# Unbroken reciprocal-root chains in the norms, one chain for the final norm, and paced reloads of expert activations, in a two-block transformer kernel

## The chip, the cores and the metric

The kernel runs on one core of one Trainium2 chip. The metric is the device time of one execution in microseconds; the median over several runs is the number compared.

## What is computed

Two blocks run one behind the other on 256 tokens of width 1024, in float32. The first has an mLSTM with a sliding-window attention beside it ("mix"), a cross attention to a memory ("cross") and a layer of 16384 experts with product keys ("peer"), and ends with a norm. The second has an "even" mixer (stick-breaking attention and retention), a convolutional feed-forward layer ("ffn0"), an "odd" mixer (gated linear attention) and a second feed-forward layer ("ffn1"). The parts that matter here, cut short:

```python
def rms_norm(x, g):
    y = xf * lax.rsqrt(jnp.mean(xf * xf, axis=-1, keepdims=True) + EPS)
    return (y * g).astype(x.dtype)

def peer_ffn(...):                       # per block of tokens, all 16384 experts by product keys
    u = expert_down[eidx]
    a = gelu(einsum('thkd,td->thk', u, xb))
    return einsum('thk,thkd->td', g * a, expert_up[eidx])

def first_block(...):
    h = h + peer_ffn(rmsnorm(h, g_ffn[l]), ...)
    return rmsnorm(h, g_final)           # the final norm

def second_block(...):
    hn = rms_norm(h, mix_norm_g[layer])  # a norm directly behind the final norm
    mix = even_mixer(hn, ...)            # p = hn @ w_in; qa = rms_norm(to_heads(sb_q), q_gain); ...
    h = h + mix
    hn = rms_norm(h, ffn_norm_g[layer])
    h = h + conv_ffn(hn, ...)
```

## The kernel before

**Weights.** Every weight matrix is cut into pieces of 512 KB, 533 of them. For each piece the SP queue issues one DMA into a tile `raw` (L423), ACT rounds it into `hi` (L438), and DVE writes the rest `raw - hi` into `lo` (L439). PE then does three matmuls for each product (`mm3`, L448 to L450: `hi` by the high part of the activations `xh`, `hi` by their low part `xl`, `lo` by `xh`; `out_step`, L586 to L588, does the same for output projections). A piece is 24 matmuls of 128x256, or 12 of 128x512 where tokens are the rows of the result. A piece lives in one of 3 weight buffers in the expert stage and of 6 in the later stages.

**Order.** A scheduler (the Tile framework) reorders the instructions of each engine; on the chip each engine runs its own list strictly in that order. `issue_after(ins)` binds instructions to stand behind `ins`.

**Norms.** A norm isn't applied to the activations before the projection; the projection runs on unscaled activations, and its results are scaled by `r`, one factor for each token. So the projection starts while `r` is still being found: squares on ACT and DVE, `sums` on PE (L200), `rsqrt` on DVE (L461 to L478: ten small operations, `rs_m` to `rs_y`), then for the stages that need `r` along the row `spread` on PE (L213, written `tp<-ident,rs_y`) and a copy on ACT (`xR`, L215). `columns` (L202) starts the sums and the chain, a few pieces into the projection; `rows` does the spread.

**The final norm** (`Final.columns`, L290) stands between the expert stage and the even stage and needs two factors: `rf` for the final norm, and `r` for the norm behind it. Two chains run one behind the other, with three multiplications between and after them.

**The even stage** computes seven projections of four pieces each (`proj_a`, 128x512 matmuls). `ev_qk` scales the first two (`y`), takes a norm by heads (`hns`, then one more chain), and defers `turn`, four transposes on PE and a copy `sb`, by `5 + t` pieces. Eight operations `x.residual(k)` (`h<-h,g,fR`) apply the final norm to `h`. There are eight PSUM banks: four named `acc`, four named `tp`. A `proj_a` takes two `acc` banks.

**The expert stage** first multiplies by `expert_down` (128 pieces), then by `expert_up` (128 pieces). While the routing is being worked out, the first 110 activations are written to memory (`store`, 55 transfers of 256 KB); in the second half they are read back (`u<-store`, L1248) and multiplied onto the routing weights (`ga<-ga,u`, L1249). The pairs of activations that were never stored come first. At the start of the second half SP also issues two single loads: `h<-spill` (1 MB, L1229) and the constants `c_late` (1089 KB, L625).

Of the kernel before, what the change touches and what calls it, by code (L numbers as in the profile page):

```python
# [10 lines left out]
F32 = mybir.dt.float32  # L11
# [6 lines left out]
ALU = mybir.AluOpType  # L18
# [3 lines left out]
P = 128  # L22
# [128 lines left out]
class Norm:  # L151
# [50 lines left out]
    def columns(self):  # L202
        ps = self.b.tp()
        self.sums(ps, "s", 0)
        self.r2 = self.b.rsqrt(ps[:, :2], 2, 1.0, keep=self.tag)
        self.r = [self.r2[:, t:t + 1] for t in range(2)]

# [48 lines left out]
class Final(Norm):  # L256
# [32 lines left out]
    def columns(self):  # L289
        b, nc = self.b, self.b.nc  # L290
        ps = b.tp()
        self.sums(ps, "s", 0)
        self.sums(ps, "f", 2)
        self.rf = b.rsqrt(ps[:, :2], 2, 1.0, keep="f")
        q = b.sp.tile([P, 2], F32, tag="fq", name="fq")
        nc.vector.tensor_mul(q, ps[:, 2:4], self.rf)
        nc.vector.tensor_mul(q, q, self.rf)
        r = b.rsqrt(q, 2, 1.0, keep=self.tag)
        nc.vector.tensor_mul(r, r, self.rf)
        self.r2 = r  # L300
        self.r = [r[:, t:t + 1] for t in range(2)]
# [70 lines left out]
class Builder:  # L372
    def __init__(self, tc, nc, A, out, stages=None):
        self.tc, self.nc, self.A, self.out = tc, nc, A, out
        self.stages = stages
        self.flip = 0
        self.gate = None
        self.free = 100
        self.later = []
        self.mark = None  # L380
        self.apart = []

# [32 lines left out]
    def weight(self, ap, width=D, parts=1):  # L415
        nc = self.nc
        i = self.wn % sum(n for _, n in self.wps)
        self.wn += 1
        wp, bufs = self.wps[0] if i < self.wps[0][1] else self.wps[1]
        raw = wp.tile([P, D], F32, tag="raw", name="raw", bufs=bufs)  # L420
        cuts = [slice(i * width // parts, (i + 1) * width // parts) for i in range(parts)]
        for c in cuts:
            nc.sync.dma_start(raw[:, c], ap[:, c])  # L423
        hi = wp.tile([P, D], F32R, tag="hi", name="hi", bufs=bufs)
        if wp not in self.apart:
            self.apart.append(wp)
            self.skip(wp, 128, "apart")
        lo = wp.tile([P, D], F32R, tag="lo", name="lo", bufs=bufs)
        with ExitStack() as ctx:
            if self.gate:  # L430
                self.free -= 1
                if self.free < 0:
                    for ins in self.gate:
                        ctx.enter_context(self.tc.issue_after(ins))
                if self.free < -4:
                    self.gate = None
            for c in cuts:
                nc.scalar.activation(hi[:, c], raw[:, c], AF.Copy)  # L438
                nc.vector.tensor_sub(lo[:, c], raw[:, c], hi[:, c].bitcast(F32))  # L439
        return hi, lo  # L440
# [17 lines left out]

    def rsqrt(self, ss, n, inv, keep=None):
        sp, v = self.sp, self.nc.vector  # L460
        ms = sp.tile([P, n], F32, tag="rs_m", name="rs_m")  # L461
        v.tensor_scalar(ms, ss, inv, EPS, op0=ALU.mult, op1=ALU.add)
        gi = sp.tile([P, n], I32, tag="rs_g", name="rs_g")
# [12 lines left out]
        out = sp.tile([P, n], F32, tag="rk_" + keep if keep else "rs_y", name="rs_y")  # L476
        v.tensor_mul(out, p, z)
        return out  # L478
# [7 lines left out]

    def proj_a(self, x, aps, width, evac):
        kk = D // width
        n = aps.shape[0]
        accs = [self.acc() for _ in range(2)]  # L490
        for p in range(n):
            wh, wl = self.weight(aps[p])
            for j in range(kk):
                k = p * kk + j
                for t in range(2):
                    sl = (slice(None), k, slice(t * P, (t + 1) * P))
                    cs = slice(j * width, (j + 1) * width)
                    self.mm3(accs[t][:, :width], x.hi[sl], x.lo[sl], wh[:, cs], wl[:, cs], k == 0, k == n * kk - 1)
            x.tick()
            self.step()  # L500
            if p < n - 1:
                yield
        for t in range(2):
            evac(t, accs[t][:, :width])
        yield
# [115 lines left out]

    def consts(self, names, arr):
        n = sum(CONST_COLS[k] for k in names)
        t = self.cp.tile([P, n], F32, tag=arr, name=arr)
        self.nc.sync.dma_start(t, self.A[arr])  # L625
        o = 0
        for k in names:
            self.c[k] = t[:, o:o + CONST_COLS[k]]
            o += CONST_COLS[k]

    def masks(self, pool, tmp, *names):
# [20 lines left out]
    def build(self):  # L652
# [17 lines left out]
        with ExitStack() as ctx:  # L670
            self.sp = self.pool(ctx, "small", bufs=2)
            self.psp = self.pool(ctx, "psum", space=PSUM)
            self.skip(self.pool(ctx, "gaps"), 64)
            self.xu = self.pool(ctx, "xu", bufs=1)
# [411 lines left out]
    def peer(self, xu, base, cw, cx, cq, late, spill, nxt):  # L1086
        nc, A = self.nc, self.A
        mm = nc.tensor.matmul
        with ExitStack() as ctx:
# [138 lines left out]
            self.h = self.pool(late, "h2", side="right").tile([P, 8, T], F32, tag="h", name="h")  # L1228
            nc.sync.dma_start(self.h, spill)  # L1229
            self.cp = self.pool(late, "c_late", side="right")  # L1230
            self.consts(LATE, "c_late")
            u1 = self.xu.tile([P, 8, T], F32R, tag="uh", name="u3")
            order = [j for j in range(0, P, 2) if j >= kept] + [j for j in range(GA, P, 2) if j < kept]
            order += [j for j in range(0, GA, 2) if j < kept]
            coef = {}

            def step(n):
                j = order[n // 2]
                if n % 2 == 0:
                    if j < GA and cg is not None and "x" not in coef:  # L1240
                        coef["x"] = True
                        cg.close()
                        self.skip(self.pool(late, "gapq2", side="right"), 64)
                        self.xq = self.pool(late, "xq2", side="right")
                    src = gslice(j, 2)
                    if j < kept:
                        a = acts_next()
                        nc.sync.dma_start(a.rearrange("p i t -> p (i t)"), store[j // 2])  # L1248
                        nc.vector.tensor_mul(src, src, a)  # L1249
                    i = 4 * (n // 2 % 2)  # L1250
# [111 lines left out]
    def even(self, x, nxt):  # L1362
        nc, A, c = self.nc, self.A, self.c
        mm = nc.tensor.matmul
        with ExitStack() as ctx:
# [9 lines left out]
            qk = [mp.tile([P, 4, T], F32, name="sb%d" % i) for i in range(2)]  # L1375

            def ev_qk(which):
                def f(t, ps):
                    y = mt.tile([P, 8, 64], F32, tag="y", name="y")
                    self.copy_r(y, ps.rearrange("p (h d) -> p h d", h=8), x.r[t])  # L1380
                    r = self.head_norm(mt, y, 8, 64, "hn")
                    nc.vector.tensor_mul(y, y, r[:, :, None].to_broadcast([P, 8, 64]))
                    y = y.rearrange("p h d -> p (h d)")
# [8 lines left out]

                    self.defer(5 + t, turn)
                return f
# [30 lines left out]
            for k in range(8):  # L1425
                self.defer(12 + 2 * k, lambda k=k: x.residual(k))
            self.run(self.proj_a(x, A["even_in"][1], 512, ev_qk(1)))
            self.run(self.proj_a(x, A["even_in"][2], 512, lambda t, ps: self.copy_r(sv[:, t], ps, x.r[t])))

# [326 lines left out]
```

## Time and profile before

| what | value |
|---|---|
| median of 3 runs | 1691.09 us |
| lowest and highest run | 1686.33 and 1693.12 us |
| the profiled execution's own time | 1694.88 us |
| its span | 1693.1 us |
| mean granted TensorE clock of the span | 0.990 |
| PE busy | 1642.2 us, 97% |
| DVE busy | 1261.4 us, 75% |
| ACT busy | 874.0 us, 52% |
| DMA, mean over the span | 188 GB/s |

PE, DVE, ACT and SP are TensorE, VectorE, ScalarE and SyncE. Busy times are shares of the span; the span is the profiled part of the execution, and the execution's own time is a little longer. Line numbers (L439) are those of the kernel before.

### The profile page before, as it was taken

To read this page: it belongs to the slowest core of one execution; us is meant where nothing else is said; L and a number is where in the kernel's file an instruction comes from. 1 tells how busy PE (TensorE), PEld (TensorE's weight loads), DVE (VectorE), ACT (ScalarE), POOL (GpSimd) and SP (SyncE) were. 2 spreads that over 40 slices of the span, in tenths; PEclk is the share of its full clock that TensorE was granted. 3 is DMA by queue.
4 is the path that set the end of the run, shared out by engine and by line. 5 is a ranking of instruction groups with operands and counts; after the bars stand their busy time and mean duration, and the time that the engine had idled before them with its cause. 6 is when DMAs were issued, how large, how long until landed. Compare 5 with 4: busy or idle time off the path is not lost.

```text
span 1693.1 us, 33034 instructions
## 1 busy us (share of the span) xinstructions
PE 1642.2 (97%) x13220; PEld 1561.2 (92%) x13220; DVE 1261.4 (75%) x2504; ACT 874.0 (52%) x1358; POOL 1.3 (0%) x16
## 2 busy tenths in 40 slices
PE   7999999999999999989999999899999999999999
PEld 7879899899999999988999998678999997799998
DVE  7686669998799985677655556877777775677775
ACT  6445455546555655444444445455555565455553
POOL 0000000000000000000000000000000000000000
PEclk9999999999999999999999999899999999999999
DMA  8433544567555555888655555433455545245551
GB/s 280 143 109 121 177 168 150 188 226 272 186 194 203 197 194 199 305 300 301 208 193 197 191 197 204 178 133 109 155 198 189 197 162 176 101 163 198 189 199 63
DMA packets 97516, 318.02 MB, mean 188 GB/s; under 512 B 11842, under 2 KB 13506, under 8 KB 96851
## 3 DMA queue, kind: packets, MB, share of 16 engines
q1 hardware_dynamic: 89154, 301.39, 51.9%
q10 hardware_dynamic: 8208, 14.52, 2.3%
q8 instruction: 104, 1.70, 0.4%
q14 instruction: 50, 0.40, 0.1%
HBM read 299.36 MB, written 16.52 MB: 187 GB/s over the span
## 4 chain that ended last, share of the span: by engine, by line
PE 79%; DVE 11%; DMA 6%; issue 2%; ACT 2%; SPq 0%; ACTq 0%; DVEq 0%
PE tp L448 10%; PE tp L450 10%; PE tp L449 10%; PE acc L587 8%; PE acc L588 8%; PE acc L586 8%; PE acc L448 5%; PE acc L449 5%; PE acc L450 5%; DVE lo L439 4%; DMA u<-store 3%; PE tp L1197 1%; PE tp L1198 1%; DVE ga L1249 1%; ACT hi L438 1%
## 5 line engine op out<-in xcount | busy, mean ns | idle before, releaser
L438 ACT ACTIVATE hi<-raw 128x1024 fp32r<-128x1024 f32 (+1 forms) x533 | 561.0, 1059 | 630.7 <-PE tp L449 227.1
L439 DVE TENSOR_TENSOR lo<-raw,hi 128x1024 fp32r<-128x1024 f32 (+1 forms) x533 | 648.8, 1219 | 284.9 <-ACT hi L438 284.2
L448 PE MATMUL tp<-xh,hi 128*128 128x256 f32 x1680 | 471.5, 281 | 0.8 <-ACT u L1212 0.8
L450 PE MATMUL tp<-xh,lo 128*128 128x256 f32 x1680 | 466.6, 278 | 3.9 <-DVE lo L439 3.8
L449 PE MATMUL tp<-xl,hi 128*128 128x256 f32 x1680 | 466.2, 278 | 0.0
L450 PEld LDWEIGHTS tp<-xh,lo 128*128 128x128 f32 x1680 | 317.3, 189 | 5.1 <-DVE lo L439 5.1
L448 PEld LDWEIGHTS tp<-xh,hi 128*128 128x128 f32 x1680 | 317.3, 189 | 1.0 <-ACT u L1212 1.0
L449 PEld LDWEIGHTS tp<-xl,hi 128*128 128x128 f32 x1680 | 317.6, 189 | 0.0
L587 PE MATMUL acc<-u,hi 128*128 128x256 f32 x1024 | 283.3, 277 | 4.5 <-DVE u L444 4.5
L588 PE MATMUL acc<-u,lo 128*128 128x256 f32 x1024 | 283.3, 277 | 4.2 <-DVE lo L439 4.2
L586 PE MATMUL acc<-u,hi 128*128 128x256 f32 x1024 | 282.7, 276 | 0.0
L587 PEld LDWEIGHTS acc<-u,hi 128*128 128x128 f32 x1024 | 192.2, 188 | 5.5 <-DVE u L444 5.5
L588 PEld LDWEIGHTS acc<-u,lo 128*128 128x128 f32 x1024 | 192.2, 188 | 5.2 <-DVE lo L439 5.2
L586 PEld LDWEIGHTS acc<-u,hi 128*128 128x128 f32 x1024 | 192.2, 188 | 0.0
L448 PE MATMUL acc<-hi,xh 128*128 128x512 f32 (+1 forms) x256 | 102.4, 402 | 8.2 <-ACT y L483 5.9
L449 PE MATMUL acc<-lo,xh 128*128 128x512 f32 (+1 forms) x256 | 101.5, 397 | 0.8 <-DVE lo L439 0.8
L450 PE MATMUL acc<-hi,xl 128*128 128x512 f32 (+1 forms) x256 | 101.0, 395 | 0.0
L586 PE MATMUL acc<-uh,hi 128*128 128x256 f32 x352 | 97.3, 277 | 0.1
L587 PE MATMUL acc<-ul,hi 128*128 128x256 f32 x352 | 97.2, 277 | 0.0
L588 PE MATMUL acc<-uh,lo 128*128 128x256 f32 x352 | 97.0, 276 | 0.0
L586 PE MATMUL acc<-oh,hi 128*128 128x256 f32 x256 | 72.1, 282 | 0.0
L587 PE MATMUL acc<-ol,hi 128*128 128x256 f32 x256 | 71.1, 278 | 0.0
(433 smaller groups left out, 2672.2 us busy)
## 6 DMA issues: line engine op xcount, KB each, us to landing
raw<-down SPq DMA_DIRECT2D x128, 512.0 KB, 3.8
raw<-up SPq DMA_DIRECT2D x128, 512.0 KB, 4.3
raw<-ffn_up SPq DMA_DIRECT2D x88, 512.0 KB, 3.5
raw<-ffn_down SPq DMA_DIRECT2D x44, 512.0 KB, 3.6
raw<-even_in SPq DMA_DIRECT2D x28, 512.0 KB, 4.2
store<-u ACTq DMA_DIRECT2D x55, 256.0 KB, 3.1
u<-store SPq DMA_DIRECT2D x55, 256.0 KB, 4.8
raw<-odd_in SPq DMA_DIRECT2D x24, 512.0 KB, 4.2
```

What stands on the lines that cost most here:

```text
L438: nc.scalar.activation(hi[:, c], raw[:, c], AF.Copy)
L439: nc.vector.tensor_sub(lo[:, c], raw[:, c], hi[:, c].bitcast(F32))
L448: mm(out, lh, rh, start=start, stop=False)
L449: mm(out, lh, rl, start=False, stop=False)
L450: mm(out, ll, rh, start=False, stop=stop)
L586: mm(out, wh[:, cs], oh, start=start and j == 0, stop=False)
L587: mm(out, wh[:, cs], ol, start=False, stop=False)
L588: mm(out, wl[:, cs], oh, start=False, stop=stop and j == 1)
L1197: mm(o, p1[:, b, :, e], hi[:, b, :, e], start=True, stop=False)
L1198: mm(o, p1[:, b, :, e], lo[:, b, :, e], start=False, stop=True)
L1249: nc.vector.tensor_mul(src, src, a)
```

## The change

1. `Norm.columns` and `Final.columns` set `rooted = 8`. `weight` counts it down with each piece, and the splits of the third to eighth piece after the chain was written are bound to stand behind `root`, the chain's last operation.
2. `Final.columns` finds both factors in one chain, over four columns in place of two.
3. The third projection of the even stage (`sv`) takes two `tp` banks; its head-norm transposes are deferred by `7 + t` pieces; the residual operations are bound behind the second normed `y`.
4. In the second half of the expert stage each `u<-store` is asked for four pairs ahead, and behind the newest weight load on SP; each multiplication stands one pair ahead of its use, behind the newest `lo` on DVE.
5. `c_late` and `h<-spill` are loaded in eight parts each, one at every fourth piece from piece 48 on.
6. A gap in SBUF grows from 64 to 128 bytes.

```diff
@@ Norm.columns
         self.r2 = self.b.rsqrt(ps[:, :2], 2, 1.0, keep=self.tag)
+        self.b.rooted = 8
@@ Final.columns
-        self.rf = b.rsqrt(ps[:, :2], 2, 1.0, keep="f")
-        q = b.sp.tile([P, 2], F32, tag="fq", name="fq")
-        nc.vector.tensor_mul(q, ps[:, 2:4], self.rf)
-        nc.vector.tensor_mul(q, q, self.rf)
-        r = b.rsqrt(q, 2, 1.0, keep=self.tag)
-        nc.vector.tensor_mul(r, r, self.rf)
+        ms = b.sp.tile([P, 4], F32, tag="fq", name="fq")
+        nc.vector.tensor_scalar(ms[:, :2], ps[:, :2], 1.0, EPS, op0=ALU.mult, op1=ALU.add)
+        nc.vector.scalar_tensor_tensor(ms[:, 2:], ms[:, :2], EPS, ps[:, 2:4], op0=ALU.mult, op1=ALU.add)
+        both = b.root_of(ms, 4, keep=self.tag)
+        b.rooted = 8
+        self.rf, r = both[:, :2], both[:, 2:]
@@ weight
-            nc.sync.dma_start(raw[:, c], ap[:, c])
+            self.loaded = nc.sync.dma_start(raw[:, c], ap[:, c]).ins
...
+            self.rooted -= 1
+            if 0 <= self.rooted < 6:
+                ctx.enter_context(self.tc.issue_after(self.root))
             for c in cuts:
                 nc.scalar.activation(hi[:, c], raw[:, c], AF.Copy)
-                nc.vector.tensor_sub(lo[:, c], raw[:, c], hi[:, c].bitcast(F32))
+                self.low = nc.vector.tensor_sub(lo[:, c], raw[:, c], hi[:, c].bitcast(F32)).ins
@@ root_of (the second part of rsqrt, now a function)
-        v.tensor_mul(out, p, z)
+        self.root = v.tensor_mul(out, p, z).ins
@@ peer, second half
-            nc.sync.dma_start(self.h, spill)
-            self.consts(LATE, "c_late")
+            refill = self.consts(LATE, "c_late", 8)
+            refill += [lambda k=k: nc.sync.dma_start(self.h[:, k], spill[:, k]) for k in range(8)]
...
+            def reload(m):
+                if m < len(order) and order[m] < kept:
+                    held[m] = acts_next()
+                    with self.tc.issue_after(self.loaded):
+                        nc.sync.dma_start(held[m].rearrange("p i t -> p (i t)"), store[order[m] // 2])
+
+            def apply(m):
+                if m in held:
+                    src = gslice(order[m], 2)
+                    with self.tc.issue_after(self.low):
+                        nc.vector.tensor_mul(src, src, held.pop(m))
+
             def step(n):
                 j = order[n // 2]
+                if n >= 48 and n % 4 == 0 and refill:
+                    with self.tc.issue_after(self.loaded):
+                        refill.pop(0)()
...
+                    p = n // 2
+                    for m in ((p + 1,) if p else (0, 1)):
+                        apply(m)
+                    for m in ((p + 4,) if p else range(5)):
+                        reload(m)
                     src = gslice(j, 2)
-                    if j < kept:
-                        a = acts_next()
-                        nc.sync.dma_start(a.rearrange("p i t -> p (i t)"), store[j // 2])
-                        nc.vector.tensor_mul(src, src, a)
@@ even
+            def add_residual(k):
+                with self.tc.issue_after(normed[1]):
+                    x.residual(k)
...
-                    self.defer(5 + t, turn)
+                    self.defer(7 + t, turn)
...
-            self.run(self.proj_a(x, A["even_in"][2], 512, lambda t, ps: self.copy_r(sv[:, t], ps, x.r[t])))
+            self.run(self.proj_a(x, A["even_in"][2], 512, lambda t, ps: self.copy_r(sv[:, t], ps, x.r[t]), self.tp))
```

Three places show how this moves instructions. The first is DVE at the norm of ffn0; `lo` is a weight split, the `rs_` names are the chain. Before:

```order
L439 TENSOR_TENSOR lo<-raw,hi 128x1024
L462 TENSOR_SCALAR rs_m<-tp 128x2
L439 TENSOR_TENSOR lo<-raw,hi 128x1024
L464 TENSOR_SCALAR rs_g<-rs_m 128x2
L439 TENSOR_TENSOR lo<-raw,hi 128x1024
L467 TENSOR_TENSOR rs_a<-rs_g 128x2
L439 TENSOR_TENSOR lo<-raw,hi 128x1024
```

Changed, the same place:

```order
L444 TENSOR_TENSOR lo<-raw,hi 128x1024
L466 TENSOR_SCALAR rs_m<-tp 128x2
L472 TENSOR_SCALAR rs_g<-rs_m 128x2
L475 TENSOR_TENSOR rs_a<-rs_g 128x2
L476 SCALAR_TENSOR_TENSOR rs_a<-rs_a,rs_m 128x2
L478 SCALAR_TENSOR_TENSOR rs_z<-rs_a,rs_g 128x2
L479 TENSOR_TENSOR rs_a<-rs_z 128x2
L480 TENSOR_TENSOR rs_a<-rs_a,rs_m 128x2
L482 SCALAR_TENSOR_TENSOR rs_p<-rs_a 128x2
L483 TENSOR_SCALAR rs_p<-rs_p 128x2
L485 TENSOR_TENSOR rs_y<-rs_p,rs_z 128x2
L444 TENSOR_TENSOR lo<-raw,hi 128x1024 x4
```

Before, a split stood between any two of the first eight chain operations; now the chain stands in one block and four splits follow it. PE's list there is the same in both kernels.

The second place is the even stage in the changed kernel, on DVE from the end of the first projection's head norm to the residuals (`sb` is the copy behind the transposes):

```order
L485 TENSOR_TENSOR rs_y<-rs_p,rs_z 128x8 x2
L444 TENSOR_TENSOR lo<-raw,hi 128x1024
L1418 TENSOR_TENSOR y<-y,rs_y 128x512 x2
L444 TENSOR_TENSOR lo<-raw,hi 128x1024 x2
L308 SCALAR_TENSOR_TENSOR h<-h,g,fR 128x256 x8
L1425 TENSOR_SCALAR sb_13116<-tp,sbg 128x4x128
```

The first split in these rows belongs to the fourth piece of the second projection and now stands behind the final norm's chain and the first head norm's; before, the splits of nine pieces stood between the operations of the final norm's first chain. The split of the third projection's first piece stands further down, behind the residuals, two `sb` copies and the second head norm. On PE, in the same place, the changed kernel has:

```order
L455 MATMUL acc<-hi,xl 128x512
L453 MATMUL acc<-hi,xh 128x512 x2
L214 MATMUL tp<-ident,rs_y 128x128 x2
L453 MATMUL tp<-hi,xh 128x512 x2
L454 MATMUL acc<-lo,xh 128x512
```

Two matmuls of the third projection (`tp<-hi,xh`) have moved ahead of the rest of the second's fourth piece, whose next matmul reads `lo`.

The third place is SP in the second half of the expert stage. Before:

```order
L423 DMA raw<-up 128x1024
L1229 DMA h<-spill 128x2048
L625 DMA c_late<-c_late 128x2178
L423 DMA raw<-up 128x1024 x3
L1248 DMA u_3262<-store 128x512 x2
L423 DMA raw<-up 128x1024 x3
L1248 DMA u_3262<-store 128x512 x2
L423 DMA raw<-up 128x1024
L1248 DMA u_3262<-store 128x512
```

Changed:

```order
L425 DMA raw<-up 128x1024 x5
L1255 DMA u_3262<-store 128x512
L425 DMA raw<-up 128x1024 x2
L1255 DMA u_3262<-store 128x512
L425 DMA raw<-up 128x1024 x2
L1255 DMA u_3262<-store 128x512
```

Before, one or two reloads followed nearly every weight load until all 55 were through, and the two large loads stood early; now one reload follows every second weight load over the whole half, and the sixteen parts stand between them.

## Rows read from the trace of the kernel before

**Rows 1.** The page: TensorE's share of the span, and the group of all `hi` splits.

```profile
PE 1642.2 (97%) x13220; PEld 1561.2 (92%) x13220; DVE 1261.4 (75%) x2504; ACT 874.0 (52%) x1358; POOL 1.3 (0%) x16
...
L438 ACT ACTIVATE hi<-raw 128x1024 fp32r<-128x1024 f32 (+1 forms) x533 | 561.0, 1059 | 630.7 <-PE tp L449 227.1
```

**Rows 2.** Waits of TensorE: what for, us in total, times, longest us.

```profile
PE tp L213 <- DVE rs_y L477: 8.6, 5, 3.4
...
PE acc L448 <- ACT y L483: 5.9, 1, 5.9
...
PE acc L587 <- DVE u L444: 4.5, 4, 1.5
PE acc L588 <- DVE lo L439: 4.2, 4, 1.7
...
PE tp L213 <- DVE mx L921: 2.5, 1, 2.5
```

**Rows 3.** Windows: us, busy of PE, PEld, DVE, ACT, POOL; clock, DMA share, GB/s.

```profile
700.00:805.00 105.00, 96.30 (x829) 94.53 (x828) 82.71 (x107) 44.97 (x51) 0.00 (x0) 1.00 0.89 302
805.00:1030.00 225.00, 225.00 (x1988) 225.00 (x1987) 127.90 (x127) 109.99 (x125) 0.00 (x0) 1.00 0.59 196
...
1073.80:1083.90 10.10, 5.76 (x15) 4.49 (x16) 8.83 (x41) 2.07 (x4) 0.00 (x0) 0.50 0.35 142
1204.40:1210.20 5.80, 5.80 (x27) 5.80 (x28) 3.69 (x9) 2.31 (x5) 0.00 (x0) 0.50 0.73 297
1514.10:1517.40 3.30, 3.30 (x18) 3.30 (x17) 2.77 (x7) 1.68 (x5) 0.00 (x0) 0.50 0.88 354
```

**Rows 4.** Timeline of VectorE at the norm of ffn0: start, us, instruction, [idle before <- releaser].

```profile
1196.36 0.15 DVE L462 TENSOR_SCALAR rs_m<-tp 128x2 f32<-128x2 f32 x1
1196.43 1.22 DVE L439 TENSOR_TENSOR lo<-raw,hi 128x1024 fp32r<-128x1024 f32 x1
...
1203.98 0.17 DVE L475 TENSOR_SCALAR rs_p<-rs_p 128x2 f32<-128x2 f32 x1
1204.18 0.16 DVE L477 TENSOR_TENSOR rs_y<-rs_p,rs_z 128x2 f32<-128x2 f32 x1
```

**Rows 5.** The same view at the norm of ffn1.

```profile
1505.02 0.15 DVE L462 TENSOR_SCALAR rs_m<-tp 128x2 f32<-128x2 f32 x1
...
1512.84 0.16 DVE L477 TENSOR_TENSOR rs_y<-rs_p,rs_z 128x2 f32<-128x2 f32 x1
```

**Rows 6.** Timeline of VectorE at the final norm and the first head norm.

```profile
1061.44 0.16 DVE L462 TENSOR_SCALAR rs_m<-tp 128x2 f32<-128x2 f32 x1 [2.41 <-PE tp L200]
...
1077.40 0.75 DVE L485 TENSOR_SCALAR y<-acc,rs_y 128x512 f32<-128x512 f32 x1
1078.78 1.28 DVE L1359 TENSOR_REDUCE hns<-hnq 128x8 f32<-128x512 f32 x2 [0.63 <-ACT hnq L1358]
...
1082.01 1.29 DVE L1382 TENSOR_TENSOR y<-y,rs_y 128x512 f32<-128x512 f32 x2
```

**Rows 7.** Timeline of TensorE around the stall of the even stage.

```profile
1070.59 0.39 PE L449 MATMUL acc<-lo,xh 128*128 128x512 f32 x1
1070.82 0.40 PE L450 MATMUL acc<-hi,xl 128*128 128x512 f32 x1
1071.52 0.71 PE L213 MATMUL tp<-ident,rs_y 128*128 128x128 f32 x4 [0.30 <-DVE rs_y L477]
1078.14 0.79 PE L448 MATMUL acc<-hi,xh 128*128 128x512 f32 x1 [5.91 <-ACT y L483]
```

**Rows 8.** Waits of the other engines that name a reload or a weight load of `expert_up`.

```profile
ACT hi L438 <- DMA raw<-up: 55.8, 32, 4.5
...
DVE ga L1249 <- DMA u<-store: 20.7, 16, 2.5
```

**Rows 9.** DMA issues: count, KB each, median us from issue to landing.

```profile
raw<-up SPq DMA_DIRECT2D x128, 512.0 KB, 4.3
...
u<-store SPq DMA_DIRECT2D x55, 256.0 KB, 4.8
```

More of the change, by code (lines that the diff above doesn't have):

```diff
@@ L380, in __init__ @@
         self.mark = None
+        self.root, self.rooted = None, 0
         self.apart = []
@@ L459, in rsqrt, with root_of @@
     def rsqrt(self, ss, n, inv, keep=None):
+        ms = self.sp.tile([P, n], F32, tag="rs_m", name="rs_m")
+        self.nc.vector.tensor_scalar(ms, ss, inv, EPS, op0=ALU.mult, op1=ALU.add)
+        return self.root_of(ms, n, keep)
+    def root_of(self, ms, n, keep=None):
         sp, v = self.sp, self.nc.vector
-        ms = sp.tile([P, n], F32, tag="rs_m", name="rs_m")
-        v.tensor_scalar(ms, ss, inv, EPS, op0=ALU.mult, op1=ALU.add)
         gi = sp.tile([P, n], I32, tag="rs_g", name="rs_g")
@@ L485, in copy_r, with proj_a @@
             self.nc.vector.tensor_scalar(out, in_, r, None, op0=ALU.mult)
-    def proj_a(self, x, aps, width, evac):
+    def proj_a(self, x, aps, width, evac, pool=None):
         kk = D // width
         n = aps.shape[0]
-        accs = [self.acc() for _ in range(2)]
+        accs = [(pool or self.acc)() for _ in range(2)]
         for p in range(n):
@@ L620, in pair, with consts @@
         return o
-    def consts(self, names, arr):
+    def consts(self, names, arr, parts=1):
         n = sum(CONST_COLS[k] for k in names)
         t = self.cp.tile([P, n], F32, tag=arr, name=arr)
-        self.nc.sync.dma_start(t, self.A[arr])
+        cuts = [slice(n * i // parts, n * (i + 1) // parts) for i in range(parts)]
+        loads = [lambda c=c: self.nc.sync.dma_start(t[:, c], self.A[arr][:, c]) for c in cuts]
         o = 0
@@ L629, in consts @@
             o += CONST_COLS[k]
+        if parts == 1:
+            loads[0]()
+        return loads
     def masks(self, pool, tmp, *names):
@@ L672, in build @@
             self.psp = self.pool(ctx, "psum", space=PSUM)
-            self.skip(self.pool(ctx, "gaps"), 64)
+            self.skip(self.pool(ctx, "gaps"), 128)
             self.xu = self.pool(ctx, "xu", bufs=1)
@@ L1235, in peer @@
             coef = {}
+            held = {}
+            def reload(m):
[8 more added lines that the diff above has]
+                        nc.vector.tensor_mul(src, src, held.pop(m))
             def step(n):
                 j = order[n // 2]
+                if n >= 48 and n % 4 == 0 and refill:
+                    with self.tc.issue_after(self.loaded):
+                        refill.pop(0)()
                 if n % 2 == 0:
@@ L1375, in even @@
             qk = [mp.tile([P, 4, T], F32, name="sb%d" % i) for i in range(2)]
+            normed = []
+            def add_residual(k):
+                with self.tc.issue_after(normed[1]):
+                    x.residual(k)
             def ev_qk(which):
@@ L1381, in f @@
                     r = self.head_norm(mt, y, 8, 64, "hn")
-                    nc.vector.tensor_mul(y, y, r[:, :, None].to_broadcast([P, 8, 64]))
+                    normed.append(nc.vector.tensor_mul(y, y, r[:, :, None].to_broadcast([P, 8, 64])).ins)
                     y = y.rearrange("p h d -> p (h d)")
@@ L1425, in even @@
             for k in range(8):
-                self.defer(12 + 2 * k, lambda k=k: x.residual(k))
+                self.defer(12 + 2 * k, lambda k=k: add_residual(k))
             self.run(self.proj_a(x, A["even_in"][1], 512, ev_qk(1)))
-            self.run(self.proj_a(x, A["even_in"][2], 512, lambda t, ps: self.copy_r(sv[:, t], ps, x.r[t])))
+            self.run(self.proj_a(x, A["even_in"][2], 512, lambda t, ps: self.copy_r(sv[:, t], ps, x.r[t]), self.tp))
             def stick():
```

## The prediction

> **What bounds the kernel now.** I read the page first: TensorE is busy for 1642.2 of 1693.1 us [rows 1]. Its matmuls are the same before and after the change, so it can only gain where PE stands still or runs at half clock, and lose where either is added. The waits of PE say what it stands still for: five waits for the chain's last operation (8.6 us), one of 5.9 us for a `y` of the even stage, eight for the factors of expert_up (4.5 and 4.2 us), one of 2.5 us at the memory's norm [rows 2]. In the windows the expert_up stage splits in two: PE loses 8.7 of 105 us while DMA runs at 302 GB/s, and nothing of 225 us at 196 GB/s [rows 3]. The other three windows stand right behind three of the waits: the granted clock is 0.50, so 1.2 of 2.4 GHz, for 5.76, 5.80 and 3.30 us of PE's work; half of that is lost: 2.9, 2.9 and 1.65 us [rows 3]. Last, the timeline of DVE tells why the chain is late: at ffn0 its first operation starts at 1196.36, a split of 1.22 us stands behind it, and the last starts at 1204.18, 7.8 us later; the last two, with nothing between, start 0.20 apart [rows 4].
>
> **The change part by part.** Durations come from the profiled execution (1694.88 us, 3.8 above the median of the runs); the sum is made against that and then moved to the median.
>
> *The norms of ffn0 and ffn1.* Ten operations at 0.20 end 2.0 us after they begin: at about 1198.4 for ffn0 and 1507.0 for ffn1, where they ended at 1204.3 and 1513.0 [rows 4, 5]. PE came to the spread 3.4 us before it could run, so at some 1201.0 and 1509.6; now it would find the chain done 2.6 us before. Both waits go, 3.4 us each [rows 2], and with them, I take it, the half clock behind them, 2.9 and 1.65 us [rows 3]. What is queued behind: the held split is late by up to 2.0 us, then four follow at 1.2 each. DVE made six splits within the chain's 7.8 us, while PE uses up three pieces in that time, so splits run ahead of PE: a piece keeps PE busy for 24 x 0.113 = 2.72 us (0.113 is 225.00 us over 1988 matmuls [rows 3]), more than the 1.2 us of a split, so DVE catches up. **-6.3 and -5.1 us**; if the clock falls all the same, -3.4 each.
>
> *Other norms.* Of the 8.6 us, 1.7 lie at the norms of cross, peer and even [rows 2]; about 1.4 of it goes with the unbroken chains of cross and peer: **-1.4**. At the memory's norm the wait of 2.5 us goes too, but a split that stood ahead of a long reciprocal there now stands behind the chain. The trace has no such wait; I bound it by the wait itself, -2.5, and a chain of 2.0 us that PE would wait out, +2.0, and take **-1.0**, nearer to the middle than to an end because both effects are sure and neither size is.
>
> *Reloads.* They were asked as early as buffers allowed: 51 in 105 us. Their late arrival shows twice: DVE waited 20.7 us for reloads and ACT 55.8 us for weight pieces [rows 8], and PE's eight waits (8.7 us) follow from either. Now one reload goes with each pair of pieces: 1.31 MB in 2 x 2.72 = 5.44 us, some 241 GB/s, over the whole half, between a stretch that lost nothing at 196 and one that lost at 302 [rows 3]. Asked at pair p for use at p + 4 and multiplied at p + 3, a reload has three pairs, 16 us, for a landing of 4.8 [rows 9]. A weight piece has 9 us from issue before PE waits: its buffer is asked anew when the old piece is split, 3 x 2.72 = 8.2 us less 2.3 for the splits [rows 1, 4] and, while PE still works on the two pieces ahead, 3.1 more; it lands in 4.3 [rows 9]. On SP a reload that waits for its buffer holds the weight loads behind it; the buffer comes free with a multiplication that stands three pairs earlier, so I cost it at nothing; if that cover went, see the second rival. The 16 small parts add 2.1 MB to some 60 pieces (163 us), 13 GB/s. The stage keeps 0 to 3.7 us of its waits: **-8.7**, at worst -5.
>
> *The even stage.* Here the change takes one wait and, by the order of DVE's list, makes two. What goes: 5.9 and 0.3 us of waiting and the 2.9 us of half clock behind [rows 2, 3, 7]. What comes: the one chain (eleven operations) begins where the first did, at 1061.44, and ends at 1063.7. Then `y`, the squares, `hns`, ten pairs of small operations come before any split. Before, `hns` began 1.4 us after `y`, and from there to the second `y` took 3.2 [rows 6]; so 1063.7 + 1.4 + 3.2 + 1.2 for the split puts `lo` of the sixth buffer's piece at 1069.5. PE, with nine matmuls of 0.23 behind the sums, the spread (0.7) and the two matmuls moved ahead, stands at some 1064.8 [rows 7]: **first wait, 4.7 us**. From 1069.5 PE has ten matmuls of that piece, two pieces of 12 (in all 34 x 0.23 = 7.8 us, about 2.5 more at half clock) and eight transposes (about 1), to 1080.8. Meanwhile DVE does two `y`, two splits, eight residuals (about 0.4 each), then `sb`, `y`, `sb` behind PE's work, the second head norm (3.2) and only then the split of the third projection: about 1080 + 2.1 + 3.2 + 1.2, so 1086.5: **second wait, 5.6 us**. The third projection then starts at 1086.6 rather than 1078.14 [rows 7]: 8.5 us later, of which about 2 is work done ahead of it (eight transposes, four matmuls); half clock behind it costs as before. So **+6.5**. Other banks for that projection do free it from `y`, but its `lo` is then what is late.
>
> Half clock behind both waits is worked out from the windows of three waits of 3.4 and 5.9 us, each followed by it [rows 2, 3]. The trace has no two such waits close together. The Trainium skill, "TensorE: Matmul & The Clock Gate", section "HAM oscillation", says that a PE whose bursts are divided by waits goes back to the low clock and pays the change at every wait, not once; this speaks against making two waits of one. By that rule the stage is at +6.5; were the clock to stay up, it would be at +1.3, and these are my bounds with +8 for a DVE list that runs later than I put it.
>
> **The sum:** -6.3 - 5.1 - 1.4 - 1.0 - 8.7 + 6.5 = -16.0. From 1694.88 that is 1678.9; from the median **1675**.
>
> **The rivals.**
> *A, the gains are eaten (1688).* The clock still falls at the two feed-forward norms (-3.4 each), the reloads keep 3.7 us of waits (-5), the memory's norm costs 2.0 and the even stage 8: with the -1.4 that is -3.2, 1688. For it: both even waits are read from DVE's list, not from a trace; against: the gains at ffn0 and ffn1 have 2.6 us to spare.
> *B, slower: weight loads late in the whole expert_up half.* Place: the split `hi` of each piece, with only three weight buffers. The early stretch lost 8.7 of 105 us, 8.3% [rows 3]; if reloads at 241 GB/s make weight pieces land late as at 302, that share over all 343 us is 28 us, 20 more than now. With the other terms (-7.3) that is +12 us: 1703. It decides when a `raw<-up` lands later than 9 us after its issue, or when a reload waits for its buffer with the next weight load behind it. Against: a median of 4.3 us even with 51 of the 55 reloads crowded together [rows 9].
> *C, it doesn't do what it says.* The held splits could make PE wait for `lo` right behind the spread at ffn0 and ffn1, as in the even stage, and the wait only changes its name: these two terms are nothing, 1686. Against: there only ten operations stand ahead of the split, not thirty.
> *D, the second even wait leaves the clock up or is hidden:* even stage at +1.3, 1670.
>
> **How the numbers follow.** A difference of 0.5%, 8.5 us, is about what a measurement of this kernel can tell from no change. My forecast, 1675, has 0.60; D 0.12, faster too; A 0.15 and C 0.05, within; B 0.08, slower. Faster: 0.60 + 0.12 = 0.72; the same: 0.15 + 0.05 = 0.20; slower 0.08. The range reaches from D with a memory norm 1.5 better and runs 3 us below their median, 1665, up to A, 1688; it leaves out B and the far ends of the others.
>
> **What would show it.** At ffn0 and ffn1 no wait of PE at the spread, clock 1.00 behind it, and the chain in about 2 us on DVE. In expert_up PE full from the first piece on, DMA near 240 GB/s over the whole half, and no wait for reloads. In the even stage two waits of PE for `lo` of about 5 us each in place of one for `y`, with clock 0.50 behind each. I am wrong if the even stage shows one short wait or three, if PE waits for splits behind the unbroken chains, or if `raw<-up` lands later than 9 us.

## The result, and the profile after the change

The changed kernel takes 1669.10 us (median of 4 runs, 1669.03 to 1672.27); beside it the kernel before took 1691.38 (4 runs, 1686.33 to 1693.12). The ratio is 0.9878, 95% interval 0.9854 to 0.9902: about 1.2% faster, 22.3 us between the medians. The forecast was 1675, with 1665 to 1688 as its range. The profiled execution took 1669.14 us.

TensorE's line of the page, against [rows 1], and its waits, against [rows 2] (what for, us in total, times, longest us):

```profile
PE 1632.5 (98%) x13220; PEld 1552.9 (93%) x13220; DVE 1262.6 (76%) x2492; ACT 874.1 (52%) x1358; POOL 1.3 (0%) x16
```

```profile
PE tp L454 <- DVE lo L444: 5.6, 1, 5.6
PE acc L454 <- DVE lo L444: 5.2, 2, 5.0
...
PE acc L455 <- DVE lo L444: 2.7, 2, 1.9
...
PE tp L214 <- DVE rs_y L485: 0.3, 1, 0.3
```

The same 13220 matmuls take 9.7 us less; 7.0 of it is half clock that is gone (PE was busy for 24.9 us at a granted clock of 0.50 before, and is for 10.8 now). The waits for `y`, for the routing factors and for the plain norms' chains are gone. Two long waits for a split, 5.6 and 5.0 us, are new, and one of 1.9 us at the memory's norm.

The windows, against [rows 3]: in the expert_up half 102 us from the first reload on and the 221 us behind them, then behind each of the two long new waits, and at the norms of ffn0 and ffn1 (us, busy of PE, PEld, DVE, ACT, POOL; clock, DMA share, GB/s):

```profile
691.50:793.50 102.00, 102.00 (x902) 102.00 (x901) 65.92 (x74) 49.90 (x57) 0.00 (x0) 1.00 0.72 237
793.50:1014.50 221.00, 221.00 (x1952) 221.00 (x1951) 148.70 (x163) 107.13 (x122) 0.00 (x0) 1.00 0.75 250
1047.40:1054.20 6.80, 5.69 (x13) 4.45 (x14) 6.80 (x11) 1.02 (x1) 0.00 (x0) 0.50 0.54 168
1064.40:1071.30 6.90, 5.14 (x12) 4.08 (x13) 6.90 (x13) 0.47 (x1) 0.00 (x0) 0.51 0.45 148
1178.00:1186.00 8.00, 7.90 (x68) 7.66 (x67) 7.05 (x18) 7.12 (x9) 0.00 (x0) 1.00 0.21 68
1484.00:1492.00 8.00, 8.00 (x72) 8.00 (x72) 7.69 (x18) 5.93 (x8) 0.00 (x0) 1.00 0.63 201
```

PE is full in both windows of the half at 237 to 250 GB/s, the clock stays up at both feed-forward norms, and it is half behind each new wait.

VectorE at the norm of ffn0, against [rows 4], in the timeline (start, us, instruction):

```profile
1182.18 0.15 DVE L466 TENSOR_SCALAR rs_m<-tp 128x2 f32<-128x2 f32 x1
...
1183.95 0.16 DVE L485 TENSOR_TENSOR rs_y<-rs_p,rs_z 128x2 f32<-128x2 f32 x1
1184.03 4.63 DVE L444 TENSOR_TENSOR lo<-raw,hi 128x1024 fp32r<-128x1024 f32 x4
```

The chain lasts 1.9 us instead of 8.0, and four splits follow. The even stage on VectorE, against [rows 6], and on TensorE, against [rows 7]:

```profile
1040.13 0.16 DVE L296 TENSOR_SCALAR fq<-tp 128x2 f32<-128x2 f32 x1 [1.09 <-PE tp L200]
...
1042.11 0.16 DVE L485 TENSOR_TENSOR rs_y<-rs_p,rs_z 128x4 f32<-128x4 f32 x1
1042.31 0.75 DVE L493 TENSOR_SCALAR y<-acc,rs_y 128x512 f32<-128x512 f32 x1
...
1047.23 1.22 DVE L444 TENSOR_TENSOR lo<-raw,hi 128x1024 fp32r<-128x1024 f32 x1
1048.37 1.29 DVE L1418 TENSOR_TENSOR y<-y,rs_y 128x512 f32<-128x512 f32 x2
1049.57 2.35 DVE L444 TENSOR_TENSOR lo<-raw,hi 128x1024 fp32r<-128x1024 f32 x2
1051.85 3.25 DVE L308 SCALAR_TENSOR_TENSOR h<-h,g,fR 128x256 f32<-128x256 f32 x8
1059.70 0.75 DVE L1425 TENSOR_SCALAR sb<-tp,sbg 128x512 f32<-128x512 f32 x1 [4.60 <-PE tp L1424]
...
1064.89 1.22 DVE L444 TENSOR_TENSOR lo<-raw,hi 128x1024 fp32r<-128x1024 f32 x1
```

```profile
1042.79 0.71 PE L453 MATMUL tp<-hi,xh 128*128 128x512 f32 x2
1048.51 0.79 PE L454 MATMUL acc<-lo,xh 128*128 128x512 f32 x1 [5.00 <-DVE lo L444]
...
1059.85 0.70 PE L453 MATMUL acc<-hi,xh 128*128 128x512 f32 x2
1066.16 0.79 PE L454 MATMUL tp<-lo,xh 128*128 128x512 f32 x1 [5.61 <-DVE lo L444]
```

The chain needs 2.1 us, but the first split behind it starts 5.0 us after its end, and the one that the third projection needs starts 17.7 us later still. PE stands in front of both.

**Stage by stage.** PE runs the same 11952 weight matmuls in both traces, the pieces in the same order. Comparing the start of the same matmul in both gives what each stage gained. (The reload row is the stretch from matmul 4800 to 5700.)

| stage | forecast, us | before to after | with that part alone |
|---|---|---|---|
| first 300 matmuls | 0 | -2.5 | |
| memory's norm | -1.0 | -1.5 | -1.5 (norm_holds) |
| cross and peer | -1.4 | -1.7 | -2.0 (norm_holds) |
| start of expert_up, reloads | -8.7 | -11.7 | -11.7 (reloads_only) |
| passage to the even stage | 0 | -3.8 | |
| even stage | +6.5 | +7.1 | |
| norm of ffn0 | -6.3 | -6.5 | -6.4 (norm_holds) |
| norm of ffn1 | -5.1 | -5.3 | -5.3 (norm_holds) |

With 0.2 us lost elsewhere that is 25.7 us, what the two profiled executions differ by (1694.88 and 1669.14).

The gains in the two rows that the forecast leaves at 0 go with half clock that the trace before had and the trace after has not: near 15.6 us, and in the passage, each time behind short waits for a weight piece. In the passage PE waited 1.71 and 0.76 us for a piece of `even_in` before, and 0.23 after. The two stretches before, and the same places after (columns as above):

```profile
14.00:21.00 7.00, 6.11 (x37) 5.91 (x38) 5.75 (x8) 5.57 (x7) 0.00 (x0) 0.76 0.80 281
1046.40:1049.80 3.40, 3.12 (x7) 2.48 (x8) 3.40 (x7) 3.40 (x7) 0.00 (x0) 0.50 0.53 177
```

```profile
13.00:20.00 7.00, 5.59 (x46) 5.39 (x47) 5.35 (x15) 6.31 (x7) 0.00 (x0) 1.00 0.72 254
1026.00:1029.80 3.80, 3.57 (x17) 2.51 (x15) 3.80 (x7) 3.77 (x8) 0.00 (x0) 1.00 0.69 253
```

### The profile page after: what moved, and what is told of

The parts are those of the page before. It is cut to its first block, busy times and chain, and to the rows that moved or that the text cites. A ratio compares the mean times of both kernels' runs of the same rounds, so it can differ in the third digit from the quotient of the medians.

```text
span 1667.4 us, 33011 instructions
## 1 busy us (share of the span) xinstructions
PE 1632.5 (98%) x13220; PEld 1552.9 (93%) x13220; DVE 1262.6 (76%) x2492; ACT 874.1 (52%) x1358; POOL 1.3 (0%) x16
## 4 chain that ended last, share of the span: by engine, by line
PE 84%; DVE 10%; ACT 3%; DMA 2%; issue 1%; SPq 0%; ACTq 0%; DVEq 0%
PE tp L453 10%; PE acc L595 10%; PE acc L594 10%; PE tp L454 10%; PE tp L455 10%; PE acc L596 10%; PE acc L454 5%; PE acc L453 5%; PE acc L455 5%; DVE lo L444 3%; ACT hi L443 1%; PE tp L1209 1%; PE tp L1210 1%; DVE w L1380 1%; DMA raw<-w_in_t 1%
## 5 line engine op out<-in xcount | busy, mean ns | idle before, releaser
L454 PE MATMUL acc<-lo,xh 128*128 128x512 f32 (+1 forms) x240 | 95.1, 396 | 5.2 <-DVE lo L444 5.2
L453 PE MATMUL acc<-hi,xh 128*128 128x512 f32 (+1 forms) x240 | 95.5, 400 | 0.0
L455 PE MATMUL acc<-hi,xl 128*128 128x512 f32 (+1 forms) x240 | 94.3, 393 | 0.0
```

The costliest lines, as they stand in the source:

```text
L453: mm(out, lh, rh, start=start, stop=False)
L454: mm(out, lh, rl, start=False, stop=False)
L455: mm(out, ll, rh, start=False, stop=stop)
```

## The experiments

Each was timed beside the kernel before on the same chip, at least four runs of each; the gap of 96 bytes was run once.

**Reloads alone.** The kernel before with points 4 and 5 of the change:

```diff
-            nc.sync.dma_start(self.h, spill)
-            self.consts(LATE, "c_late")
+            refill = self.consts(LATE, "c_late", 8)
+            refill += [lambda k=k: nc.sync.dma_start(self.h[:, k], spill[:, k]) for k in range(8)]
...
+                    for m in ((p + 1,) if p else (0, 1)):
+                        apply(m)
+                    for m in ((p + 4,) if p else range(5)):
+                        reload(m)
```

> The kernel before with the paced reloads and the parted loads alone (points 4 and 5 of the change). My theory: the expert_up half starts with PE full and gains the 11.7 us that the traces of before and after differ by between its first and its 900th matmul; the rest of the trace stays as before, with the 5.9 us wait for y and the 3.4 us waits at both feed-forward norms. Time: 1691.4 less 11.7, about 1680. Rival: the 3.8 us that the start of the even stage gained in the changed kernel also belong to the reloads (weight pieces of even_in land earlier when the queue is quiet), then 1676, and PE has no wait for raw of even_in at the end of the half. Second rival: spreading the reloads does not do it, and the 20 us were won elsewhere: over 1688.

Measured: 1677.05 us, ratio 0.9916 (0.9891 to 0.9941). Matmuls 4800 to 5700 gain 11.7 us, and the other waits stay:

```profile
PE tp L213 <- DVE rs_y L477: 8.2, 5, 3.4
...
PE acc L448 <- ACT y L483: 5.9, 1, 5.9
```

The theory holds for the half itself. The medians differ by 14.6 us; the interval (some 10 to 18 us) takes in 11.7. The passage to the even stage gained 2.7 here, but it gained 3.0 in norm_holds, where no reload was touched, and 0.6 in later_heads5, whose reloads are the same as here: it goes with the execution, not with the reloads. Half clock stands in the passage in the trace before and in those of later_heads5 and third_in_acc, which gain 0.6 and 0.7 there; in the other eleven there is none, and they gain 2.5 to 4.0.

**Hold behind the final norm away.**

```diff
         both = b.root_of(ms, 4, keep=self.tag)
-        b.rooted = 8
```

> The changed kernel, but the splits behind the final norm are not held; its one chain, the third projection's banks and the bound residuals stay. My theory: the two waits of the even stage (5.0 and 5.6 us) are made by the hold, which puts the head norm ahead of the splits. Without it eight splits stand between the chain's operations again, the chain ends at about 10.6 us after it began instead of 2.2, but PE's list has the spread 42 matmuls (9.7 us) behind the sums, so PE waits there about 1 us, and it does not wait for y, because the third projection has other banks. Both half-clock stretches go too, some 2.9 us each: 1669.1 - 10.6 - 5.8 + 1, about 1654. Rival: the late chain makes PE wait for y all the same, as before the change (5.9 us and 2.9 of half clock): then within 6 us of the changed kernel, 1663 to 1672.

Measured: 1657.22 us, ratio 0.9799 (0.9775 to 0.9824), 12 us less than the changed kernel. The timelines of VectorE and TensorE at the final norm:

```profile
1044.25 0.16 DVE L296 TENSOR_SCALAR fq<-tp 128x2 f32<-128x2 f32 x1 [1.10 <-PE tp L200]
1044.33 1.22 DVE L444 TENSOR_TENSOR lo<-raw,hi 128x1024 fp32r<-128x1024 f32 x1
...
1054.31 0.16 DVE L485 TENSOR_TENSOR rs_y<-rs_p,rs_z 128x4 f32<-128x4 f32 x1
```

```profile
1054.53 0.71 PE L214 MATMUL tp<-ident,rs_y 128*128 128x128 f32 x4 [0.53 <-DVE rs_y L485]
```

The chain is slow again, 10.2 us, and it costs 0.53 us, since PE has 42 matmuls to do meanwhile. From matmul 7800 to 8250 this kernel gains 8.4 us on the one before, where the changed kernel loses 7.1: 15.5 us, as the theory had it. The whole differs by less because the first 300 matmuls of its trace, which the edit doesn't touch, took 4.5 us longer, with half clock in them. The hold is what cost.

**Third projection back in acc banks.**

```diff
-            self.run(self.proj_a(x, A["even_in"][2], 512, lambda t, ps: self.copy_r(sv[:, t], ps, x.r[t]), self.tp))
+            self.run(self.proj_a(x, A["even_in"][2], 512, lambda t, ps: self.copy_r(sv[:, t], ps, x.r[t])))
```

> The changed kernel, but the third even projection takes acc banks again. My theory: in the changed kernel these banks are worth next to nothing, since with the hold what is late is the split of the third projection and not the banks: y is ready before PE comes to it. Only the two matmuls that stand ahead of the first wait come some 0.3 us later. Time within 2 us of the changed kernel, 1669. Rival: the banks carry the gain of the even stage, and PE waits for y as before: 5 us or more longer, 1674 or over.

Measured: 1670.62 us, ratio 0.9879 (0.9854 to 0.9903), the same as the changed kernel within the noise. On TensorE:

```profile
1064.72 0.72 PE L453 MATMUL acc<-hi,xh 128*128 128x512 f32 x2 [0.85 <-ACT y L491]
1069.93 0.80 PE L454 MATMUL acc<-lo,xh 128*128 128x512 f32 x1 [4.49 <-DVE lo L444]
```

PE waits 0.85 us for `y` and then 4.49 for the split: 5.3 in place of 5.6. With the hold the banks are worth nothing that shows in the time.

**The hold, but four splits ahead of the head norm.**

```diff
-            self.run(self.proj_a(x, A["even_in"][0], 512, ev_qk(0)))
+            self.run(self.proj_a(x, A["even_in"][0], 512, lambda t, ps: self.defer(5, lambda: ev_qk(0)(t, ps))))
```

The second projection likewise; the transposes are deferred by `2 + t`, so they stand where they stood.

> The changed kernel with the hold, but the two head norms of the even stage are written five pieces later (their transposes as late as before), so that the unbroken chain is followed by four splits and only then by the head norm. My theory: what is wrong with the hold is not the unbroken chain but what else overtakes the splits; with four splits first, both waits and both half-clock stretches go: 1669.1 - 10.6 - 5.8, about 1653. Rival: DVE is short of time in this stretch whatever the order, and the wait moves to a later split or to the transposes of a later head norm: 1660 to 1669, with a new wait of some us between 1048 and 1075 us.

Measured: 1659.02 us, ratio 0.9809 (0.9783 to 0.9835). The waits of 5.0 and 5.6 us shrink to 0.20 and 0.56, one of 0.98 for transposes appears at 1078.75, and matmuls 7800 to 8250 gain 5.1 us on the kernel before: both half-clock stretches are gone, as the theory has it, and the rival's wait of some us doesn't come. But without any hold the same stretch gained 8.4; here PE still idles for 2.8 us in it, in six short waits, and there for 0.5. So most of the cost, 12.2 of 15.5 us, comes from what overtakes the splits behind the unbroken chain, and what is left of it goes with small waits.

**One chain or other banks.** Without the hold behind the final norm: one chain with acc banks (the two edits above together), and then two chains with tp banks (the diff shows the second, cut):

```diff
-        both = b.root_of(ms, 4, keep=self.tag)
-        b.rooted = 8
...
+        self.rf = b.rsqrt(ps[:, :2], 2, 1.0, keep="f")
...
+        r = b.rsqrt(q, 2, 1.0, keep=self.tag)
```

> The changed kernel without the hold behind the final norm (1657.2 as measured) and with the third even projection in acc banks: one chain alone. My theory: the one chain ends as PE comes to the spread (it waited 0.5 us there), the first y follows in 0.7 us, and PE asks for the acc banks at just that moment, so it waits at most 1 to 1.5 us: 1657 to 1660. Rival: the banks are what takes the wait away, and PE waits 3 us or more for y, with half clock behind: 1663 or over.

Measured: 1655.17 us, ratio 0.9784 (0.9768 to 0.9801), the fastest median of all. TensorE waits 0.53 us for the chain and 0.48 for `y`:

```profile
1054.84 0.71 PE L214 MATMUL tp<-ident,rs_y 128*128 128x128 f32 x4 [0.53 <-DVE rs_y L485]
1056.03 0.50 PE L453 MATMUL acc<-hi,xh 128*128 128x512 f32 x1 [0.48 <-ACT y L491]
```

> The same, but with the two chains of before and the third projection in tp banks: the banks alone. My theory: the second chain makes y 2.5 to 4 us later, but PE has four pieces (11 us) that need neither y nor its banks, so that no wait is left: 1656 to 1659, as with both. Rival: the transposes or the fourth projection, which does take the acc banks, come to wait for the later y: 1661 or over, with a wait of over 2 us behind the spread.

Measured: 1679.17 us, ratio 0.9925 (0.9909 to 0.9942): neither theory nor rival. No new wait stood in the even stage. The matmuls themselves were slower over most of the kernel. My edit had kept point 6, the larger SBUF gap, which belongs to one chain: one chain needs 64 bytes less in the pool of small tiles, and the gap of 128 instead of 64 leaves all tiles behind it where they were. With two chains the weights had moved up by 64 bytes. So the run was repeated with the gap of 64:

> The kernel two_chains_tp once more, with the SBUF gap of 64 bytes that belongs to two chains. In the run before, the gap of 128 had moved the weight tiles from addresses that are 0 modulo 128 to 64 modulo 128, which is where xh and xl lie; matmuls then stood 0.117 to 0.118 us apart instead of 0.113 wherever weights meet xh, and not in the expert_up half, where both operands had moved. My theory: that alone made it slow; with weights at 0 again it is as good as one chain: 1655 to 1659, pace 0.113 throughout. Rival: the second chain itself costs in the even stage or elsewhere: 1662 or over.

Measured: 1659.33 us, ratio 0.9821 (0.9804 to 0.9838). Either the one chain or the other banks takes the wait for `y` away; from matmul 7800 to 8250 they gain 7.8 and 6.8 us alone and 8.4 together (no_final_hold).

**Point 6 undone alone,** the gap of 64 bytes in the changed kernel, and then a gap of 96:

```diff
-            self.skip(self.pool(ctx, "gaps"), 128)
+            self.skip(self.pool(ctx, "gaps"), 64)
```

> The changed kernel with the gap of 64 bytes as before: point 6 undone alone. One chain needs 64 bytes less in the small pool, so all tiles behind it move down by 64, the weights to 64 modulo 128, as xh and xl. My theory: PE's pace depends on where the two operands of a matmul lie relative to each other: 0.117 to 0.118 us per matmul in all stages but expert_up, and some 20 us (what two_chains_tp lost, 22 us, in the same stages): 1688 to 1692, the whole gain gone. Rival: addresses do not matter and two_chains_tp was slow for its second chain: 1669.

> The changed kernel with a gap of 96 bytes: weights at 96 modulo 128, xh and xl at 64, so 32 apart. If only an equal place modulo 128 is slow, the pace is 0.113 and the time 1669; if what counts is being 64 apart, it is 0.117 and some 1690; between them, a graded loss.

Measured: with 64 bytes 1697.24 us, ratio 1.0047 (1.003 to 1.0064), slower than the kernel before, and a loss larger than the theory's 20 us; with 96 bytes 1694.24 in the single run. Windows of a hundred microseconds (columns as above): ffn0 in the changed kernel; ffn0 and then the expert_up half with the gap of 64; ffn0 with the gap of 96; and ffn0 in two_chains_tp:

```profile
1200.00:1300.00 100.00, 100.00 (x885) 100.00 (x884) 75.28 (x114) 53.08 (x75) 0.00 (x0) 1.00 0.63 202
```

```profile
1220.00:1320.00 100.00, 100.00 (x851) 100.00 (x850) 72.09 (x108) 50.06 (x71) 0.00 (x0) 1.00 0.59 190
860.00:960.00 100.00, 100.00 (x884) 100.00 (x884) 66.94 (x75) 48.66 (x55) 0.00 (x0) 1.00 0.79 255
```

```profile
1220.00:1320.00 100.00, 100.00 (x858) 100.00 (x857) 72.29 (x108) 50.69 (x71) 0.00 (x0) 1.00 0.59 189
```

```profile
1210.00:1310.00 100.00, 100.00 (x860) 100.00 (x859) 72.51 (x108) 50.69 (x71) 0.00 (x0) 1.00 0.59 189
```

PE is fully busy at full clock in all five. In ffn0 it does 885 matmuls in 100 us in the changed kernel, 851 with the gap of 64, 858 with 96 and 860 in two_chains_tp. In the built programs of before and after the weights start at addresses that are 0 modulo 128, and the activations `xh` and `xl` at 64; with the gap of 64 the weights are at 64 too, with 96 at 96. In expert_up both operands lie behind the gap and moved together: 884 matmuls, no loss. So what counts is how the two operands lie to each other, and not where either lies. Modulo 128 they are 64 bytes apart in the fast kernels, and 0 or 32 apart in the slow ones. But the distance modulo 128 is not the whole rule: in two_chains_tp the weights are at 64 too, 64 bytes above their place in the changed kernel, where the gap of 64 puts them 64 below it, and the pace is another, 860 against 851.

**Lead and parts of the reloads.** First `c_late` and `h` as single early loads, then each reload asked two pairs ahead:

```diff
-            refill = self.consts(LATE, "c_late", 8)
-            refill += [lambda k=k: nc.sync.dma_start(self.h[:, k], spill[:, k]) for k in range(8)]
+            nc.sync.dma_start(self.h, spill)
+            refill = self.consts(LATE, "c_late")[:0]
```

```diff
-                    for m in ((p + 4,) if p else range(5)):
+                    for m in ((p + 2,) if p else range(3)):
```

> The changed kernel, but c_late and h are loaded by one transfer each at the start of the expert_up half again; reloads stay paced. My theory: the 11.7 us come from pacing the 55 reloads; the two large loads together are 2.1 MB, about 17 us of landing one after the other, and delay one or two weight pieces: 0 to 3 us back, 1669 to 1672. Rival: the large loads early in the half were a main cause of the late weight pieces: 5 us or more back, 1674 or over.

> The changed kernel, but each reload is asked two pairs ahead in place of four, and still multiplied one pair ahead: one pair, 5.4 us, is left for a landing that took 4.8 in the kernel before. My theory: what helped is the even pace and not the lead; with the queue quiet the landing is shorter than 4.8 and PE loses 0 to 2 us more: 1669 to 1671. Rival: the lead is what keeps DVE from waiting; then every reload that lands over 5 us after its issue holds the splits behind it, some of 55 cost 0.5 to 1 us each: 1674 or over, and DVE waits for reloads appear again.

Measured: 1672.13 us, ratio 0.9887 (0.9871 to 0.9904), and 1671.63, ratio 0.9881 (0.9864 to 0.9897). Both keep the whole 11.7 us between matmul 4800 and 5700; what their traces are slower by, 3.0 us each, lies for the most part in the first 300 matmuls (2.8 and 2.9), which the edits don't touch. With single loads ACT waited once, without PE noticing it:

```profile
ACT hi L443 <- DMA raw<-up: 3.6, 1, 3.6
```

The even pace alone makes the gain; neither a lead of four pairs over one of two nor the parting is worth anything that shows here.

**The plain norms' hold alone** in the kernel before, with the count in `weight` as in the change:

```diff
         self.r2 = self.b.rsqrt(ps[:, :2], 2, 1.0, keep=self.tag)
+        self.b.rooted = 8
```

> The kernel before with the hold of the splits behind each plain norm (point 1 without the final norm) and nothing else. My theory: 6.5 us at the norm of ffn0, 5.3 at ffn1, some 2.5 at cross and peer and 1.5 at the memory's norm, as the traces of before and after differ by; the even stage and the expert_up half as before: 1691.7 less 15 to 16, about 1676. Rival: part of that came from what ran ahead of these norms in the changed kernel (other places of DVE's list after the even stage): under 8 us, 1684 or over.

Measured: 1677.94 us, ratio 0.9932 (0.9913 to 0.9951). The norms gain what the theory says (last column of the table), 15.3 us in all. Between the medians it is 11.4 us faster and not 15: in its trace the crowded reloads lost 4.2 us more than in the trace before, without an edit there, most of it in two stretches of half clock (at 733 and 784 us) that the trace before hasn't:

```profile
PE acc L592 <- DVE u L449: 7.8, 4, 3.0
...
PE acc L593 <- DVE lo L444: 2.4, 3, 1.1
```

## Why the prediction was right, step by step

- *The norms of ffn0 and ffn1.* As worked out: -6.5 and -5.3 against -6.3 and -5.1, the half clock included. PE did not wait for the splits behind the chain, so rival C falls; the clock stayed up, so rival A, which needs it to fall here, falls too.
- *Other norms.* -1.7 against -1.4. At the memory's norm the wait for the split came, 1.95 us, and the stage still gained 1.5, or 0.5 to 0.6 in the traces where half clock stood behind it (third_in_acc, later_heads5, late_ask, one_chain_acc); inside the bounds.
- *Reloads.* The mechanism was right and the size too small: -11.7 against -8.7. The step that failed is "PE loses 8.7 of 105 us", read from its busy time. A matmul is recorded as 0.28 us long while the next starts 0.113 us later, so up to 0.17 us of every stop counts as busy. By count, 829 matmuls at 0.1132 are 93.8 us, and 11.2 of the 105 were lost. The median landing of a reload fell from 4.8 to 3.8 us and that of `raw<-up` from 4.3 to 3.6 ([rows 9], and the lines below for the changed kernel), so rival B falls: the half lost nothing at 250 GB/s.

```profile
raw<-up SPq DMA_DIRECT2D x128, 512.0 KB, 3.6
...
u<-store SPq DMA_DIRECT2D x55, 256.0 KB, 3.8
```

- *The even stage.* +7.1 against +6.5, out of waits of 5.00 and 5.61 us where 4.7 and 5.6 stood. Half of 5.69 and of 5.14 us is lost to the clock behind them, 2.8 and 2.6. The Trainium skill, "TensorE: Matmul & The Clock Gate", section "HAM oscillation", has the change paid at every wait, and this trace agrees: 0.50 and 0.51 in the two windows. Rival D falls, although the time, 1669, is nearer to its 1670 than to the forecast's 1675: the second wait came, with half clock behind it.
- *The gap in SBUF.* The prediction passed over it, at no cost and without naming what hides it. In the change it is indeed neutral, but only because it makes up for 64 bytes that the one chain frees; without it the kernel is at 1697 (after_gap64). That it cost nothing was luck, not argument.
- *The sum.* The terms that belong to the change came to -19.6 against -16.0. The rest, -6.1, lies in two places where I had no term: the first 300 matmuls, which moved by -2.5 to +2.0 from trace to trace in kernels that hold the first norm alike, and the passage to the even stage, where a weight load of `even_in` lands sooner or later (-0.6 to -4.0). Both go with half clock: after, norm_holds and third_in_acc have none in the first 300 matmuls and gain 2.2 to 2.5 there, and no_final_hold, with 10.3 us of it, loses 2.0. Why the loads land sooner in some executions is not settled. The profiled execution before was also 3.5 us above its median, so of the 22.3 us between the medians only 2.7 lie outside the terms.

The changed kernel is faster in spite of its hold at the final norm: the kernels here that drop the hold, with the weights in their place, take 1655 to 1659 us, another 10 to 14 us. Of its point 3, the other banks add nothing to the one chain (1657 with both, 1655 with acc banks); the new places of its residual operations and transposes were not tested alone.

## What to carry over

Before binding work behind a short chain on an in-order engine, look at what else becomes ready when the chain ends: here the hold paid where only ten operations stood ahead of the splits, and cost 15 us where a whole head norm slipped in between. A transfer that isn't urgent is asked for at the pace at which it is used; crowding 55 reloads together cost 11.7 us, and 15.9 in another execution. When a tile's size changes, compare the addresses of all tiles behind it before and after.

## What the runs showed of the hardware that was not expected

A matmul's pace depends on where its two operands lie in SBUF relative to each other. From start to start, over the same 1100 matmuls of ffn0 (8400 to 9500), it was 0.1133 us with weights and activations 64 bytes apart modulo 128, 0.1169 at 32 bytes apart, and at the same place modulo 128 once 0.1179 (after_gap64) and once 0.1167 (two_chains_tp), at full granted clock and with PE shown 100% busy. Over this kernel the gap of 64 cost 28 us, more than the 22.3 us that the whole change gained. Only these four placements were tried; the rule behind them is open.

The same short wait is not always followed by half clock. At the memory's norm PE waits 1.93 to 1.99 us for a split in all twelve traces that hold that norm; the granted clock behind it is 0.50 in six of them and stays at 1.00 in the other six, and the stage gains 0.5 or 1.5 us accordingly.
